# The opening of an encoder trunk: a modulation sum set between two products, and the second half of the tokens squared and partly normed before the last product

## The chip, the cores and the metric

The kernel runs as one program on one core of a Trainium2 chip. A core has a matrix engine (TensorE, PE in the profile, with its weight loads as PEld), a vector engine (VectorE, DVE), an activation engine (ScalarE, ACT), GpSimd (POOL) and SyncE (SP), which here only issues transfers. Each engine works through its own instructions in order and waits for the others by semaphores. The metric is the device time of one execution in microseconds, lower is better.

## The reference

Two layers of a transformer-like encoder over 1024 tokens of width 1024, all in float32, and a final RMS norm. In each layer the tokens are normed and modulated, projected once into the queries, keys and values of three attention groups (A: a 2-D neighbourhood, B: a sliding window, C: dense, with a norm per head and a rotation), the groups' outputs are projected back, and a gated feed-forward network follows. What the change touches is the first layer's first line and the part of the projection that makes group C's queries and keys:

```python
cond = jax.nn.silu(c)
for l in range(DEPTH):
    mod = cond @ w_mod[l] + b_mod[l]
    sh_a, sc_a, gt_a, sh_f, sc_f, gt_f = [m[:, None, :] for m in split_cols(mod, (D,) * 6)]
    h = rms_norm(x, g_attn[l]) * (1 + sc_a) + sh_a
    proj = h @ w_in[l]
    ...
```

So before any product with `h` can run, the shift `sh_a` and the scale `sc_a` have to be had from a vector-matrix product over `w_mod`, and the tokens have to be read, squared and summed.

## The kernel before

Width is cut into 8 blocks of 128 (index n), tokens into 8 tiles of 128 (index t) and two halves of 512. `xt` holds the tokens turned, block by block: 128 channels on the partitions, tokens along the row. `hh` and `hl` hold the normed and modulated `h` as two float32r parts, a rounded one and its remainder, and every weight is split in the same way (`whi` by ScalarE, `wlo` by VectorE or POOL). One product of a block and a tile is therefore three matmuls (`mm3`: hi with hi, lo with hi, hi with lo), accumulated in a PSUM tile. The pool of these tiles holds eight (`bufs=8`), called banks here; all the tiles named ps_... below take one each and take turns in them.

The opening, ahead of the loop over layers, is written out by hand in one order, and `pin` keeps the instructions of TensorE, ScalarE, VectorE and SP in the order of the code. Its pieces:

- `gm_load(i)`, `gemv_half(i)`: the modulation of the first layer comes in four pairs of blocks, p = 0 to 3, each from two loads (i = 2p and 2p+1). Of each load VectorE adds up three rows into `ga`, and TensorE takes the fourth straight into the bank `ps_mod`; at the second load TensorE also sums `ga` over the partitions there, and ScalarE copies the row out (`gr`).
- `gemv_turn(p)`, `gemv_finish(p)`: TensorE turns that row to partitions (`ps_m`), VectorE adds the bias and makes the gain (`vecs`).
- `h_blocks(half, rows, ns)`: for the blocks in ns, VectorE makes `nt` (tokens times gain times 1/rms), ScalarE adds the shift and rounds (`hh`), VectorE makes the remainder (`hl`). `pair_done(p)` is the turn, the finish and the two blocks of the first half of the tokens.
- `c_first(n)`: block n of the C product for the first four tiles, twelve matmuls into four banks `ps_c` that stay taken to the end of the opening. In this document C product n means that call.
- `x_load`, `x_square`, `x_rms`, `x_turn`, `spread`: the tokens of a half are loaded as four tiles `xn`; ScalarE squares them with a running sum (`xt,rx<-xn`; what it writes to `xt` is thrown away) and takes the root, VectorE the reciprocal; TensorE turns each block (`ps_x`) and ScalarE copies it to `xt`; `spread` turns the four columns of 1/rms to rows (`ps_r`). For the first half those rows are copied to `rb`, for the second they are read from the bank.
- `w_split`: the next pair of C weight blocks split; `spill`: `xt` stored to device memory by SP; `turn_vecs`: the second layer's vectors turned (`pst`); `c_norm_first`: the start of the C norm of token tile 0 (`gm`, `cq`, then POOL's rotation `ct`).

The layer's loop then begins with the C product of token tiles 4 and 5, which needs the second half's `hh` and `hl`, and goes on with the A and B projections (`ps_ab`, weights split by VectorE and later by POOL), the C norms of tiles 1 to 7 (`csq`, `r`, `cq`, `ct`, `qn`) and the turns of the normed tiles (`pq`, `pk`). The order of VectorE, ScalarE and POOL is pinned there too.

All engine calls pass through one recording helper, so nearly every row of the profile says L49; the tiles' names tell the rows apart.

Of the kernel before, what the change touches and what calls it, by code (L numbers as in the profile page):

```python
# [10 lines left out]
F32 = mybir.dt.float32  # L11
# [8 lines left out]
P = 128  # L20
D = 1024
S = 1024
KC = D // P
# [62 lines left out]
def trunk(ctx: ExitStack, tc, A, C, out):  # L86
# [358 lines left out]
    def spread(r, j0, psp, tag="mm"):  # L445

        ps = psp.tile([P, 512], F32, name="ps_r", tag=tag)
        for j in range(4):
            pe.transpose(
                ps[:, j * P : (j + 1) * P], bc(r[:, j0 + j : j0 + j + 1], [P, P]), ident  # L450
            )
        return ps
# [83 lines left out]
    st_cm, stp = open_pool("start", side="right")  # L536
# [32 lines left out]
    def x_rms(r):  # L569
        act.activation(r, r, AF.Sqrt, bias=epst, scale=1.0 / D)  # L570
        dve.reciprocal(r, r)

    def x_turn(half, xn, ns, engines):

        c = slice(half * H, (half + 1) * H)
        for n in ns:
            ps = psl.tile([P, 512], F32, name="ps_x", tag="mm")
            for i in range(4):
                pe.transpose(
                    ps[:, i * P : (i + 1) * P], xn[i][:, n * P : (n + 1) * P], ident  # L580
                )
            if engines[n % 2] is act:
                act.copy(xt[:, n, c], ps)
            else:
                dve.tensor_copy(xt[:, n, c], ps)
# [23 lines left out]
            rows = A["w_mod"][0, r0 : r0 + 4 * P, c0 : c0 + 2 * P]  # L609
            sp.dma_start(gm[:, :, g, :], rows.rearrange("(k p) n -> p k n", p=P))  # L610

    def gemv_half(i):
        p, s = i // 2, i % 2
        gm = gms.pop(i).rearrange("p k g n -> p k (g n)")
        if s == 0:
            gas[p] = stp.tile([P, 4 * P], F32, name="ga", tag="ga", bufs=2)
            gps[p] = psl.tile([P, 4 * P], F32, name="ps_mod", tag="mm")
        ga, row = gas[p], gps[p][0:1]
        for k in range(3):
            mod_add(4 * s + k, ga, gm[:, k])  # L620
        pe.matmul(row, condT[:, 4 * s + 3 : 4 * s + 4], gm[:, 3], start=(s == 0), stop=False)
        if s:
            pe.matmul(row, ones, ga, start=False, stop=True)
            gas[p] = stp.tile([1, 4 * P], F32, name="gr", tag="gr", bufs=1)
            act.copy(gas[p], row)

    def gemv_turn(p):

        ps = gps[p] = psl.tile([P, 4], F32, name="ps_m", tag="mm")
        row = gas.pop(p)  # L630
        for c in range(4):
            pe.transpose(ps[:, c : c + 1], row[:, c * P : (c + 1) * P], ident[0:1, 0:1])

    def gemv_finish(p):

        ns = slice(2 * p, 2 * p + 2)
        m, v = (t[:, 0:16].rearrange("p (g n) -> p g n", g=2) for t in (mods[0], vecs[0]))
        dve.tensor_tensor(
            out=m[:, :, ns], in0=gps.pop(p).rearrange("p (g n) -> p g n", g=2),
            in1=v[:, :, ns], op=ALU.add,  # L640
        )
        dve.scalar_tensor_tensor(
            out=gsc[0][:, ns], in0=m[:, 1, ns], scalar=1.0,
            in1=vecs[0][:, 48 + 2 * p : 50 + 2 * p], op0=ALU.add, op1=ALU.mult,
        )

    def h_blocks(half, rows, ns):

        c = slice(half * H, (half + 1) * H)
        ts = {}  # L650
        for n in ns:
            t = ts[n] = stp2.tile([P, H], F32, name="nt", tag="nt", bufs=3)
            dve.scalar_tensor_tensor(
                out=t, in0=xt[:, n, c], scalar=gsc[0][:, n : n + 1], in1=rows,
                op0=ALU.mult, op1=ALU.mult,
            )
        for n, t in ts.items():
            act.activation(hh[:, n, c], t, AF.Identity, bias=mods[0][:, n : n + 1])
        for n, t in ts.items():
            dve.scalar_tensor_tensor(  # L660
                out=hl[:, n, c], in0=t, scalar=mods[0][:, n : n + 1], in1=f32(hh[:, n, c]),
                op0=ALU.add, op1=ALU.subtract,
            )
# [4 lines left out]
            sp.dma_start(dst, v)  # L668
        wcs.append(st)

    def c_first(n):

        wh, wl = wC[n // 2]
        for t in range(T0):
            ts_ = slice(t * P, (t + 1) * P)
            mm3(
                pssC[t], hh[:, n, ts_], hl[:, n, ts_], wh[:, n % 2], wl[:, n % 2],
                n == 0, n == KC - 1,
            )
# [52 lines left out]
    def pair_done(p):  # L732
        gemv_turn(p)
        gemv_finish(p)
        if p == 0:
            keep_busy(8)
        h_blocks(0, rb, (2 * p, 2 * p + 1))
# [39 lines left out]
    pair_done(2)  # L777
    x_square(1, 1, xns[1][1], rxs[1])
    c_first(4)
    c_first(5)  # L780
    w_split()
    wab.append(w_ab(0, 1))
    spill(0)
    gemv_half(7)
    pair_done(3)
    for j in (2, 3):
        x_square(1, j, xns[1][j], rxs[1])
    x_rms(rxs[1])
    x_turn(1, xns[1], range(4), (act, act))
    c_first(6)  # L790
    x_turn(1, xns[1], range(4, KC), (act, act))
    c_first(7)
    spill(1)
    rows = spread(rxs[1], 0, psl)
    turn_vecs(1, v1)
    gm = stp.tile([P, 2048], F32, name="gm", tag="gm", bufs=3)
    first_t1 = c_norm_first(pssC[0], gm[:, 0:512], gm[:, 512:1024], gm[:, 1024:1032])
    for n in range(0, KC, 2):
        h_blocks(1, rows, (n, n + 1))
    sp.dma_start(sinkc, bc(A["sink_sw"].rearrange("l h -> (l h)")[None, :], [P, 12]))  # L800
    for l in range(2):
# [1551 lines left out]
```

## Time and profile before

| | |
|---|---|
| median of 3 runs | 2461.02 us (2459.26 to 2463.18) |
| the profiled execution | 2460.37 us, its span 2458.6 us |
| mean granted TensorE clock | 0.991 |
| busy share TensorE, VectorE, ScalarE, POOL | 97%, 74%, 50%, 31% |
| the opening ends and the layer begins | about 71 us |

Read it so: a row of a timeline has the start and the duration in microseconds, engine, line, operation, the tile written and those read, partitions x elements, how often, and in brackets the idle time ahead of it with what ended it. Rows with x2 or more are merged from neighbours that ran one behind the other. Matmul durations overlap, so the distance from one start to the next is what one costs. All times are from the start of the span.

### The profile page before, as it was taken

The numbers are of one execution on the slowest core, as the hardware profiler recorded it, in microseconds if no ns is written. First come the engines' busy times: TensorE is split into PE (matmuls) and PEld (weight loads), VectorE is DVE, ScalarE is ACT, GpSimd is POOL, SyncE is SP. The second block draws the span as 40 slices with busy tenths as digits, with TensorE's granted clock in tenths as the row PEclk, the third lists the DMA queues.
The fourth block names the chain that finished last, engine by engine and source line by source line (L and its number), as shares of the span: only waits on it lengthen the run. The fifth ranks groups of instructions, "written<-read, shape, count | busy, mean of one in ns | idle before, by whom it ended". The sixth has DMA issues, their size and how long they took to land.

```text
span 2458.6 us, 34285 instructions
## 1 busy us (share of the span) xinstructions
PE 2390.3 (97%) x12005; PEld 1992.7 (81%) x12005; DVE 1821.8 (74%) x2966; ACT 1224.9 (50%) x2306; POOL 764.3 (31%) x769
## 2 busy tenths in 40 slices
PE   8999999999999999999999999999999999999998
PEld 5787899878788877788887789987887888888886
DVE  5757999877967878587677679999698555446865
ACT  3422888954543333344544148888454333333443
POOL 1520444620244444300036114465005434430001
PEclk9999999999999999999999999999999999999999
DMA  8468205245345454496433851151624332229743
GB/s 287 147 177 287 54 14 146 57 151 167 95 142 173 158 168 140 154 287 201 129 116 106 259 195 27 41 152 44 210 90 141 125 115 95 99 102 283 215 134 110
DMA packets 285206, 356.04 MB, mean 145 GB/s; under 512 B 32997, under 2 KB 201533, under 8 KB 285033
## 3 DMA queue, kind: packets, MB, share of 16 engines
q1 hardware_dynamic: 277816, 341.12, 44.6%
q10 hardware_dynamic: 6912, 12.59, 1.6%
q8 instruction: 95, 1.56, 0.3%
q14 instruction: 79, 0.64, 0.1%
q0 software_dynamic: 304, 0.14, 0.0%
HBM read 269.62 MB, written 86.69 MB: 145 GB/s over the span
## 4 chain that ended last, share of the span: by engine, by line
PE 71%; DVE 11%; DMA 6%; issue 5%; ACT 4%; POOL 2%; SPq 1%; ACTq 0%; POOLq 0%; DVEq 0%
PE ps_w L49 30%; PE ps_d L49 10%; PE ps_o L49 7%; PE pv L49 6%; PE ps_ab L49 5%; PE T L49 4%; PE sC L49 3%; DVE wpt L49 2%; DMA wmt<-in_w_mod_dram 2%; PE ps_c L49 1%; ACT pr L49 1%; DMA zt<-skA 1%; PE sA L49 1%; DMA zAd<-zt 1%; DMA w<-in_w_down_dram 1%
## 5 line engine op out<-in xcount | busy, mean ns | idle before, releaser
L49 PE MATMUL ps_d<-wpt 128*128 128x512 f32 x1848 | 425.3, 390 | 2.0 <-DVE wpt L49 0.7
L49 PEld LDWEIGHTS ps_d<-wpt 128*128 128x128 f32 x1848 | 345.4, 188 | 77.2 <-DVE wpt L49 3.1
L49 POOL TENSOR_SCALAR pr<-pr,rs 128x1024 f32<-128x1024 f32 (+4 forms) x252 | 207.6, 826 | 308.5 <-DVE rs L49 290.7
L49 POOL TENSOR_TENSOR sg<-sg,u 128x512 f32<-128x512 f32 x86 | 124.2, 1445 | 360.9 <-ACT sg L49 228.0
L49 PE MATMUL pv<-pt,vs 128*128 128x256 f32 x1216 | 202.5, 297 | 8.0 <-DVE rs L49 2.3
L49 DVE TENSOR_TENSOR pt<-T,pt 128x512 fp32r<-128x512 f32 x304 | 199.4, 680 | 11.4 <-ACT pt L49 9.9
L49 ACT CAST pt<-T 128x512 fp32r<-128x512 f32 x304 | 170.2, 586 | 44.5 <-PE T L49 42.8
L49 PE MATMUL T<-identr,pr 128*128 128x128 f32 x1288 | 187.6, 273 | 2.2 <-ACT rb L49 1.0
L49 ACT COPY u<-ps_w 128x512 f32<-128x512 f32 x128 | 75.2, 587 | 215.1 <-PE ps_w L49 215.1
L49 PEld LDWEIGHTS pv<-pt,vs 128*128 128x128 f32 x1216 | 161.7, 190 | 23.2 <-DVE y L49 7.6
L49 DVE SCALAR_TENSOR_TENSOR acc<-wmt,condT,acc 128x512 f32<-128x512 f32 (+1 forms) x98 | 115.0, 1183 | 84.5 <-DMA wmt<-in_w_mod_dram 84.2
L49 DVE TENSOR_TENSOR wpt<-w,wpt 128x512 fp32r<-128x512 f32 x154 | 111.2, 722 | 84.0 <-ACT wpt L49 83.9
L49 PEld LDWEIGHTS T<-identr,pr 128*128 128x128 f32 x1288 | 153.1, 141 | 21.9 <-issue 3.2
L49 POOL TENSOR_TENSOR wpt<-ws,wpt 128x512 fp32r<-128x512 f32 x80 | 112.3, 1405 | 181.5 <-ACT wpt L49 139.3
L49 ACT CAST wpt<-w 128x512 fp32r<-128x512 f32 x154 | 95.5, 620 | 134.2 <-PE ps_d L49 127.9
L49 ACT CAST wpt<-ws 128x512 fp32r<-128x512 f32 x176 | 107.8, 622 | 56.4 <-issue 22.4
L49 ACT CAST wpt<-graw 128x512 fp32r<-128x512 f32 x154 | 95.0, 617 | 74.6 <-DMA graw<-gpd 65.2
L49 DVE TENSOR_TENSOR wpt<-ws,wpt 128x512 fp32r<-128x512 f32 x96 | 85.1, 895 | 59.1 <-ACT wpt L49 59.0
L49 DVE TENSOR_REDUCE rs<-sC 128x1 f32<-128x1024 f32 x96 | 116.4, 1218 | 6.4 <-PE sC L49 5.9
L49 DVE TENSOR_TENSOR wpt<-graw,wpt 128x512 fp32r<-128x512 f32 x154 | 110.4, 717 | 10.5 <-ACT wpt L49 10.4
L49 PE MATMUL ps_w<-ht3h,wpt 128*128 128x512 f32 x352 | 111.8, 399 | 6.4 <-ACT sg L49 6.4
L49 DVE TENSOR_TENSOR ws<-wr 128x512 f32<-128x512 f32 x88 | 78.8, 898 | 51.7 <-POOL wpt L49 48.7
(287 smaller groups left out, 6027.3 us busy)
## 6 DMA issues: line engine op xcount, KB each, us to landing
wr<-in_w_gu_dram SPq DMA_DIRECT2D x92, 512.0 KB, 4.2
gpd<-sg SPq DMA_DIRECT2D x154, 256.0 KB, 4.4
graw<-gpd SPq DMA_DIRECT2D x76, 512.0 KB, 3.7
w<-in_w_down_dram SPq DMA_DIRECT2D x110, 256.0 KB, 5.2
wmt<-in_w_mod_dram SPq DMA_DIRECT2D x48, 512.0 KB, 5.9
qk<-qkd SPq DMA_DIRECT2D x44, 512.0 KB, 7.3
wst<-in_w_o_dram SPq DMA_DIRECT2D x32, 512.0 KB, 3.5
wmt<-in_w_mod_dram SPq DMA_DIRECT2D x64, 256.0 KB, 3.5
```

The source lines that it names most:

```text
L49: ins = op(*args, **kwargs)
```

## The change

It moves calls of the opening's hand-written order and splits two functions so that they can be called in pieces.

1. `gemv_half(7)`, the last modulation sum, is called between C products 4 and 5, and without its copy; the copy (`gemv_row`), the turn and the finish are called apart, and C product 5 is issued as two pieces of two token tiles, one ahead of the turn and one behind it.
2. The last two squares of the second tokens and their root and reciprocal stand ahead of that copy.
3. The spread of their 1/rms stands ahead of C product 6.
4. Their blocks 0 and 1 are normed behind product 6, blocks 2 and 3 behind product 7, and only blocks 4 to 7 behind the start of the C norm.

```diff
--- before.py
+++ after.py
@@ -609,7 +609,7 @@
             rows = A["w_mod"][0, r0 : r0 + 4 * P, c0 : c0 + 2 * P]
             sp.dma_start(gm[:, :, g, :], rows.rearrange("(k p) n -> p k n", p=P))
 
-    def gemv_half(i):
+    def gemv_half(i, copy=True):
         p, s = i // 2, i % 2
         gm = gms.pop(i).rearrange("p k g n -> p k (g n)")
         if s == 0:
@@ -621,8 +621,13 @@
         pe.matmul(row, condT[:, 4 * s + 3 : 4 * s + 4], gm[:, 3], start=(s == 0), stop=False)
         if s:
             pe.matmul(row, ones, ga, start=False, stop=True)
-            gas[p] = stp.tile([1, 4 * P], F32, name="gr", tag="gr", bufs=1)
-            act.copy(gas[p], row)
+            if copy:
+                gemv_row(p)
+
+    def gemv_row(p):
+        row = gps[p][0:1]
+        gas[p] = stp.tile([1, 4 * P], F32, name="gr", tag="gr", bufs=1)
+        act.copy(gas[p], row)
 
     def gemv_turn(p):
 
@@ -668,10 +673,10 @@
             sp.dma_start(dst, v)
         wcs.append(st)
 
-    def c_first(n):
+    def c_first(n, ts=None):
 
         wh, wl = wC[n // 2]
-        for t in range(T0):
+        for t in ts or range(T0):
             ts_ = slice(t * P, (t + 1) * P)
             mm3(
                 pssC[t], hh[:, n, ts_], hl[:, n, ts_], wh[:, n % 2], wl[:, n % 2],
@@ -777,25 +782,31 @@
     pair_done(2)
     x_square(1, 1, xns[1][1], rxs[1])
     c_first(4)
-    c_first(5)
+    gemv_half(7, copy=False)
     w_split()
     wab.append(w_ab(0, 1))
     spill(0)
-    gemv_half(7)
-    pair_done(3)
     for j in (2, 3):
         x_square(1, j, xns[1][j], rxs[1])
     x_rms(rxs[1])
+    gemv_row(3)
+    c_first(5, (0, 1))
+    gemv_turn(3)
+    c_first(5, (2, 3))
+    gemv_finish(3)
+    h_blocks(0, rb, (6, 7))
     x_turn(1, xns[1], range(4), (act, act))
+    rows = spread(rxs[1], 0, psl)
     c_first(6)
+    h_blocks(1, rows, (0, 1))
     x_turn(1, xns[1], range(4, KC), (act, act))
     c_first(7)
     spill(1)
-    rows = spread(rxs[1], 0, psl)
+    h_blocks(1, rows, (2, 3))
     turn_vecs(1, v1)
     gm = stp.tile([P, 2048], F32, name="gm", tag="gm", bufs=3)
     first_t1 = c_norm_first(pssC[0], gm[:, 0:512], gm[:, 512:1024], gm[:, 1024:1032])
-    for n in range(0, KC, 2):
+    for n in (4, 6):
         h_blocks(1, rows, (n, n + 1))
     sp.dma_start(sinkc, bc(A["sink_sw"].rearrange("l h -> (l h)")[None, :], [P, 12]))
     for l in range(2):
```

What that does on the engines is shown at three places. First TensorE, at C product 5, with the buffers' numbers left in (ps_c_297 to ps_c_300 are the four tiles' banks). Before, the end of product 5 and what follows:

```order
L49 MATMUL ps_c_299<-whi_405,hh_106 128x512
L49 MATMUL ps_c_299<-whi_405,hl_107 128x512
L49 MATMUL ps_c_299<-wlo_406,hh_106 128x512
L49 MATMUL ps_c_300<-whi_405,hh_106 128x512
L49 MATMUL ps_c_300<-whi_405,hl_107 128x512
L49 MATMUL ps_c_300<-wlo_406,hh_106 128x512
L49 MATMUL ps_mod_435<-gm_360,condT_84 1x512
L49 MATMUL ps_mod_435<-ga_434,onesr_78 1x512
L49 MATMUL ps_m_501<-identr_68,gr_499 128x1 x4
```

And in the changed kernel, the same place, which now begins right behind product 4:

```order
L49 MATMUL ps_mod_435<-gm_360,condT_84 1x512
L49 MATMUL ps_mod_435<-ga_434,onesr_78 1x512
L49 MATMUL ps_c_297<-whi_405,hh_106 128x512
L49 MATMUL ps_c_297<-whi_405,hl_107 128x512
L49 MATMUL ps_c_297<-wlo_406,hh_106 128x512
L49 MATMUL ps_c_298<-whi_405,hh_106 128x512
L49 MATMUL ps_c_298<-whi_405,hl_107 128x512
L49 MATMUL ps_c_298<-wlo_406,hh_106 128x512
L49 MATMUL ps_m_499<-identr_68,gr_491 128x1 x4
L49 MATMUL ps_c_299<-whi_405,hh_106 128x512
```

The sum `ps_mod` stands ahead of the product and the turn `ps_m` in its middle; the turned blocks `ps_x` follow the product at once.

Second VectorE, from the remainder of the fifth and sixth block on (the difference, - before and + after; `ga` is the sum over loads, `wlo` the weight split, `ps_r` the spread 1/rms of the second tokens):

```order
-L49 TENSOR_TENSOR wlo<-wst,whi 128x1024
 L49 SCALAR_TENSOR_TENSOR ga<-gm,condT,ga 128x512 x3
+L49 TENSOR_TENSOR wlo<-wst,whi 128x1024
+L49 RECIPROCAL rx<-rx 128x4
 L49 TENSOR_TENSOR vecs_85<-ps_m,vecs_85 128x2x2
 L49 SCALAR_TENSOR_TENSOR vecs_85<-vecs_85 128x2
 L49 SCALAR_TENSOR_TENSOR nt<-xt,vecs_85,rb 128x512 x2
 L49 SCALAR_TENSOR_TENSOR hl<-nt,vecs_85,hh 128x512 x2
-L49 RECIPROCAL rx<-rx 128x4
+L49 SCALAR_TENSOR_TENSOR nt<-xt,vecs_85,ps_r 128x512 x2
+L49 SCALAR_TENSOR_TENSOR hl<-nt,vecs_85,hh 128x512 x2
```

The three additions of the last load have passed the weight split, the reciprocal has passed the finish of the last pair, and the second tokens' blocks stand right behind the first tokens' last ones.

Third ScalarE, from the split of the last C weights on (`xt,rx<-xn` are the squares, `xt<-ps_x` the copies of turned blocks):

```order
 L49 CAST whi<-wst 128x1024
+L49 ACTIVATE xt,rx<-xn 128x2x512 x2
+L49 ACTIVATE rx<-rx,epst 128x4
 L49 COPY gr<-ps_mod 1x512
 L49 ACTIVATE hh<-nt,vecs_85 128x512 x2
-L49 ACTIVATE xt,rx<-xn 128x2x512 x2
-L49 ACTIVATE rx<-rx,epst 128x4
-L49 COPY xt<-ps_x 128x512 x8
+L49 COPY xt<-ps_x 128x512 x4
+L49 ACTIVATE hh<-nt,vecs_85 128x512 x2
+L49 COPY xt<-ps_x 128x512 x4
+L49 ACTIVATE hh<-nt,vecs_85 128x512 x2
```

The squares and the root have passed the copy `gr`, and the eight copies of turned blocks have the second tokens' `hh` between and behind them. SP's transfers and POOL's instructions keep their order.

## The prediction

> **What bounds the kernel now.** First the page: TensorE is busy nearly throughout, so a gain must come from the places where it waits.
>
> ```profile
> span 2458.6 us, 34285 instructions
> ...
> PE 2390.3 (97%) x12005; PEld 1992.7 (81%) x12005; DVE 1821.8 (74%) x2966; ACT 1224.9 (50%) x2306; POOL 764.3 (31%) x769
> ```
>
> Then a table by stage of the opening and of the layer's start, cut where the chain of waits changes hands; the columns are the stretch and its length, the busy time of TensorE, its weight loads, VectorE, ScalarE and POOL (with instructions), the granted clock, the DMA share and GB/s. It shows which engine is full: ScalarE in 62 to 71, VectorE in 71 to 86 while TensorE holes, TensorE again from 116.8 to 142.2.
>
> ```profile
> 62.00:71.00 9.00, 8.60 (x45) 6.59 (x45) 1.58 (x3) 7.49 (x15) 0.00 (x0) 1.00 0.72 268
> 71.00:86.20 15.20, 10.41 (x36) 7.95 (x35) 14.16 (x22) 6.49 (x10) 4.71 (x4) 0.78 0.41 133
> 86.20:116.80 30.60, 29.87 (x156) 24.38 (x154) 25.64 (x43) 13.26 (x35) 20.64 (x18) 1.00 0.44 118
> 116.80:142.20 25.40, 25.40 (x136) 21.27 (x137) 21.16 (x29) 9.98 (x21) 16.50 (x13) 1.00 0.39 113
> ```
>
> Third, TensorE's timeline through the opening. The reader is to see the order (C product 4 to row 54.15, product 5, the last modulation sum and its turn, four turned blocks, product 6, four turned blocks, product 7, spread, vectors) and where it stands still: 0.72 before 59.60, 0.29 inside product 6, 4.41 before 75.48, 0.73 before 116.78.
>
> ```profile
> 54.15 0.39 PE L49 MATMUL ps_c<-whi,hh 128*128 128x512 f32 x1
> 57.00 1.02 PE L49 MATMUL ps_mod<-gm,condT 128*1 128x512 f32 x2
> 59.60 0.40 PE L49 MATMUL ps_m<-identr,gr 1*128 1x1 f32 x4 [0.72 <-ACT gr L49]
> 59.94 1.97 PE L49 MATMUL ps_x<-identr,xn 128*128 128x128 f32 x16
> 62.79 0.50 PE L49 MATMUL ps_c<-whi,hl 128*128 128x512 f32 x1 [0.29 <-DVE hl L49]
> 65.69 2.12 PE L49 MATMUL ps_x<-identr,xn 128*128 128x128 f32 x16
> 67.57 0.48 PE L49 MATMUL ps_c<-whi,hh 128*128 128x512 f32 x1
> 70.41 0.60 PE L49 MATMUL ps_r<-identr,rx 128*128 128x128 f32 x4
> 70.84 0.23 PE L49 MATMUL pst<-identr,v 72*128 72x72 f32 x1
> 75.48 0.79 PE L49 MATMUL ps_c<-whi,hh 128*128 128x512 f32 x1 [4.41 <-ACT hh L49]
> 89.59 0.39 PE L49 MATMUL ps_ab<-hh,whi 128*128 128x512 f32 x1
> 95.03 0.79 PE L49 MATMUL pq<-identr,qn 128*128 128x128 f32 x8
> ```
>
> ```profile
> 116.78 0.50 PE L49 MATMUL ps_ab<-hh,wlo 128*128 128x512 f32 x1 [0.73 <-POOL wlo L49]
> ```
>
> The 4.41 us are VectorE's: after the last product it runs the start of the first C norm (71.25 to 73.93) and only then the second tokens' four pairs of blocks (nt, then hl, 73.93 to 86.25). The table's casts (t5h, 86.25), the next weight split and everything after it stand behind them in VectorE's order.
>
> ```profile
> 60.44 1.42 DVE L49 SCALAR_TENSOR_TENSOR nt<-xt,vecs,rb 128x512 f32<-128x512 f32 x2
> 71.25 0.68 DVE L49 TENSOR_REDUCE gm<-gm 128x8 f32<-128x512 f32 x1
> 73.93 1.40 DVE L49 SCALAR_TENSOR_TENSOR nt<-xt,vecs,ps_r 128x512 f32<-128x512 f32 x2
> 77.66 1.39 DVE L49 SCALAR_TENSOR_TENSOR nt<-xt,vecs,ps_r 128x512 f32<-128x512 f32 x2
> 80.51 1.40 DVE L49 SCALAR_TENSOR_TENSOR nt<-xt,vecs,ps_r 128x512 f32<-128x512 f32 x2
> 86.25 0.15 DVE L49 CAST t5h<-t 32x6 fp32r<-32x6 f32 x1
> 91.92 1.44 DVE L49 TENSOR_TENSOR qn<-ct,qn 128x384 fp32r<-128x384 f32 x2 [0.77 <-ACT qn L49]
> ```
>
> **The change part by part.** No instruction is added or removed and no transfer changes its place in SP's or POOL's order; all is order on TensorE, VectorE and ScalarE. ScalarE's rows there now:
>
> ```profile
> 50.71 1.03 ACT L49 CAST whi<-wst 128x1024 fp32r<-128x1024 f32 x1
> 58.97 0.58 ACT L49 COPY gr<-ps_mod 1x512 f32<-1x512 f32 x1 [7.23 <-PE ps_mod L49]
> 62.52 1.05 ACT L49 ACTIVATE xt<-xn 128x1024 f32<-128x1024 f32 x1
> 64.87 0.30 ACT L49 ACTIVATE rx<-rx,epst 128x4 f32<-128x4 f32 x1
> 65.07 3.98 ACT L49 COPY xt<-ps_x 128x512 f32<-128x512 f32 x8
> 68.88 0.67 ACT L49 ACTIVATE gm<-ps_c 128x512 f32<-128x512 f32 x1
> 74.70 1.38 ACT L49 ACTIVATE hh<-nt,vecs 128x512 fp32r<-128x512 f32 x2 [2.44 <-DVE nt L49]
> ```
>
> *Edit 1, the sum between products.* Its two multiplies move from 57.00 to just behind product 4, 54.15 plus some 0.1. VectorE's three ga steps now stand ahead of the split, so the sum is not late. By rows 57.00 and 58.97 the copy gr starts 1.97 after the first multiply, 56.2, and ends 0.63 later (59.60 less 58.97), 56.85. TensorE meanwhile runs two tiles of product 5: 56.0 to 57.4 (2.85 for twelve matmuls by 57.00 less 54.15). The turn ps_m starts at 57.45 without the 0.72 wait: 2.15 earlier than 59.60. nt follows 0.84 later (60.44 less 59.60), 58.3; hl is whole for its first block 2.35 after nt (62.79 less 60.44), at 60.65. The turn (0.40), the other two tiles (1.4) and the turned blocks (1.97, row 59.94) run on TensorE till 61.3, so the hole before 62.79 goes too.
>
> *Edit 2, squares and 1/rms ahead of gr.* The two squares and the root (62.52 to the first copy at 65.07: 2.55) go to where ScalarE is free, behind the split of 50.71, in the 7.23 that row 58.97 waited; so they end at about 54.4, ahead of 56.2. Their cover is that idle; without it gr would be late by what they overrun. They leave the copies xt, which then start behind the two hh: 58.3, 0.77 for the first nt (74.70 less 73.93 below) and 1.38, so at 60.4 in place of 65.07.
>
> *Edit 3, spread ahead of product 6.* The spread's four turns cost TensorE 0.43 (70.41 to 70.84) and move from behind product 7: nothing in the sum of TensorE's work. They need one bank, freed by the first copy at about 61.0; TensorE is there at 61.3. Product 6 runs 61.75 to 64.5 (2.75: twelve at 0.23). The next turned blocks have three free banks rather than four, since the spread holds one to the end; a copy takes 0.5 (3.98 for eight), a block's turns 0.47 (1.88 for four, 65.69 to 67.57), so the fourth block finds the first bank free: nothing, at worst 0.6. They end at 66.45, product 7 ends 2.84 later (67.57 to 70.41), 69.3, and the turn of the vectors, now directly behind, starts at 69.35 against 70.84: 1.5 earlier.
>
> *Edit 4, blocks 0 to 3 normed early.* Two of the four VectorE pairs move into 62 to 69.3, where VectorE is 1.58 busy in 9.00. What they queue ahead of: ScalarE's hh stands between the copies, so the copies of blocks 4 to 7 wait for nt, and hh of blocks 2, 3 for the copies. The first two nt start when the spread has ended, 61.9; their hh run from 62.7 to 64.1, when no block is turned yet. The last copy ends 0.6 after the last turned block, 67.1; hh of blocks 2 and 3 take 1.38 behind it, to 68.5; the last hl ends 0.8 later, 69.3, when TensorE just gets there and has twelve matmuls of blocks 0 and 1 ahead. The square of the C norm ends 0.67 behind hh (row 68.88), 69.15, against VectorE's need of it at 69.75. That is the thinnest cover of the change, 0.6 us; ScalarE's busy 7.49 in 9.00 becomes about 8. From 69.75 VectorE runs as from 71.25, with two pairs: the first costs 3.73 beside POOL's rotation (73.93 to 77.66), the second 2.87 like the last two now (80.51 to 86.25 for both). The step of row 86.25 then comes 1.5 + 5.74 earlier (the vectors' 1.5, and the two pairs gone, 80.51 to 86.25): **7.2 us**.
>
> *What TensorE makes of it.* It starts on the second tokens at 69.5 and needs 48 matmuls (89.59 less 75.48 now) at 2.85 per twelve, 11.4, plus some 0.5 for hl of block 5: 81.3 against 89.59, 8.3 earlier. That is 1.1 more than VectorE gives. The half clock of 77 to 81 is not in these rows' rate and falls away with the hole before it. The turn of the first normed tile (95.03) now has 1.67 to spare behind VectorE's qn (91.92 plus 1.44); 0.6 stay. From there to 116 the longest of VectorE's waits in total is for ScalarE's qn, behind its own rows; the others are under half a us:
>
> ```profile
> DVE qn L49 <- ACT qn L49: 3.9, 5, 0.8
> ```
>
> So that stretch moves as one by 7.2 with POOL's split at its end; TensorE, 8.3 early, meets it with a wait of 0.73 + 1.1, about 1.8: this is where the rest of its lead is late next. Behind it TensorE is full (25.40 of 25.40), and the stage after that starts from its last turn, as the chain of waits has it:
>
> ```profile
> 141.40 0.63 PE pq L49 x8
> 142.24 0.35 SPq L49
> ```
>
> No transfer there hangs on anything but that turn, so the shift is kept to the end.
>
> **The sum.** 1.5 + 5.74 = 7.2 off the profiled execution's 2460.37 (span 2458.6 and 1.8 around it): 2453.2. The median of the runs is 0.65 above that execution, so 2453.8. Bounds: if VectorE did not hold the stretch to 116, TensorE's 8.3 and the 0.73 would count, 9.0; if the early pairs brought nothing, 1.5 stays.
>
> [...] TensorE was given half its clock twice in the opening.
>
> ```profile
> 47.00:49.20 2.20, 0.21 (x4) 0.12 (x3) 1.80 (x5) 0.82 (x2) 0.00 (x0) 1.00 0.15 38
> 50.60:54.00 3.40, 3.40 (x10) 2.66 (x9) 2.19 (x3) 1.15 (x3) 0.00 (x0) 0.50 0.19 52
> 77.30:81.30 4.00, 4.00 (x11) 3.09 (x10) 3.87 (x7) 1.39 (x3) 1.58 (x1) 0.50 0.48 148
> 193.00:200.00 7.00, 4.63 (x21) 3.53 (x20) 6.86 (x10) 0.60 (x1) 0.29 (x2) 1.00 1.05 343
> ```
>
> The first time came behind an idle time of 2 us with narrow sums ahead of it; a hole of as long in 193 to 200 (4.63 busy in 7.00) brought none. The second, behind the 4.41 wait, should vanish; the split and turn that follow were VectorE's to release, so I count nothing for it. The new hole of 1.8 is a doubt: by the row of 50.60 it could cost 3.40 x 0.5 = 1.7, so 2455.5; by that of 193 nothing. [...]
>
> **The rivals.** *The stretch behind 86 does not follow.* If something other than VectorE's order sets POOL's split, such as the weight rows that SP loads there, only 1.5 is kept: 2459.5. For it: the DMA share of 0.44 and a chain that passes through loads. Against: VectorE's list above has no DMA in it, and it is busy 25.64 of 30.60. *TensorE sets that stretch*: 9.0, 2452.0; against it is the 0.73 wait on POOL that is there already. [...]
>
> **How the numbers follow.** 0.2% is 4.9 us, about what a measurement of this kernel tells from no change. Chances: the forecast 0.62 (2453.8, itself within some 2 us by the runs' spread of 2459.26 to 2463.18), TensorE sets the stretch 0.06, a half-clock window in the new hole 0.05, the stretch does not follow 0.19, half clock throughout or slower otherwise 0.08. The first three are faster, 0.73; the fourth is the same; the last is slower. The range goes from 2450.0 (TensorE's case less 2) to 2459.8, which leaves out the slower case and the upper half of the fourth; the likeliest alone would be 2451.5 to 2456.
>
> **What would show it.** ps_m near 57.5, ps_r near 61.3, no TensorE wait of over 1 us from there to the second tokens' end; VectorE's t5h near 79; the wait for POOL's split grown to nearly 2 us; the mA load near 135. I am wrong if the early hh hold back the copies (a TensorE wait at the turned blocks), if the C norm's square comes late, or if the wait for POOL's split stays near 116.

## The result and the profile after

| | before | changed |
|---|---|---|
| median of the runs side by side (11 and 11) | 2457.29 us (2454.73 to 2463.18) | 2451.34 us (2445.28 to 2458.39) |
| ratio of the runs, 95% interval | 1 | 0.997 [0.9959, 0.998] |
| the same against 18 and 19 other runs of before | 1 | 0.9962 [0.9945, 0.998], 0.9973 [0.9959, 0.9987] |
| span of the profiled execution | 2458.6 us | 2445.4 us |
| its mean granted clock | 0.991 | 0.995 |

By the ratio the change takes 7.4 us off (0.003 of 2457.3; 4.9 to 10.1). The spans differ by 13.2, and that is not all the change: by difference some 6 us of it belong to these two executions (the last section). All runs of this study taken together give 2457.9 us as the mean of before (100 runs, standard error 0.35) and 2451.35 as that of the changed kernel (31 runs, 0.69): 6.5 us, uncertain by 0.8.

The page of the changed kernel, to be held against the span line and busy line of before:

```profile
span 2445.4 us, 34284 instructions
...
PE 2382.9 (97%) x12005; PEld 1989.4 (81%) x12005; DVE 1820.0 (74%) x2966; ACT 1224.5 (50%) x2306; POOL 763.6 (31%) x769
```

The table by stage, cut at the same places of the program (first turned blocks, second tokens' product, the step t5h, POOL's split, the mA load; columns as before):

```profile
58.50:67.20 8.70, 8.70 (x55) 7.54 (x54) 6.50 (x10) 7.50 (x14) 0.00 (x0) 1.00 1.06 402
67.20:77.00 9.80, 9.62 (x42) 7.21 (x40) 9.09 (x16) 3.82 (x6) 4.76 (x4) 1.00 0.74 250
77.00:106.90 29.90, 28.54 (x150) 23.23 (x148) 24.95 (x43) 13.13 (x35) 20.85 (x18) 1.00 0.45 122
106.90:132.40 25.50, 25.50 (x136) 21.37 (x137) 21.27 (x29) 10.12 (x21) 16.49 (x13) 1.00 0.39 114
```

The stage that was 15.20 long with TensorE 10.41 busy at a clock of 0.78 is now 9.80 long, with 9.62 busy at 1.00. VectorE's 6.50 busy in the first row (it was 1.58) come mostly from the two block pairs that came forward. The third stage's TensorE idle is its wait at POOL's split. TensorE's rows, from the sum behind product 4 on:

```profile
52.35 1.20 PE L49 MATMUL ps_mod<-gm,condT 128*1 128x512 f32 x2
55.91 0.40 PE L49 MATMUL ps_m<-identr,gr 1*128 1x1 f32 x4
57.73 1.91 PE L49 MATMUL ps_x<-identr,xn 128*128 128x128 f32 x16
59.48 0.62 PE L49 MATMUL ps_r<-identr,rx 128*128 128x128 f32 x4
62.70 1.93 PE L49 MATMUL ps_x<-identr,xn 128*128 128x128 f32 x16
67.23 0.23 PE L49 MATMUL pst<-identr,v 72*128 72x72 f32 x1
67.25 0.48 PE L49 MATMUL ps_c<-whi,hh 128*128 128x512 f32 x1
79.07 0.39 PE L49 MATMUL ps_ab<-hh,whi 128*128 128x512 f32 x1
...
106.88 0.50 PE L49 MATMUL ps_ab<-hh,wlo 128*128 128x512 f32 x1 [1.36 <-POOL wlo L49]
```

No row has a wait until 106.88 (one of 0.2 within the second tokens' product apart): the 0.72, the 0.29 and the 4.41 are gone, and the wait at POOL's split has grown from 0.73 to 1.36. VectorE at the same place:

```profile
60.20 1.40 DVE L49 SCALAR_TENSOR_TENSOR nt<-xt,vecs,ps_r 128x512 f32<-128x512 f32 x2 [0.50 <-PE ps_r L49]
66.03 1.42 DVE L49 SCALAR_TENSOR_TENSOR hl<-nt,vecs,hh 128x512 fp32r<-128x512 f32 x2 [1.56 <-ACT hh L49]
67.64 0.68 DVE L49 TENSOR_REDUCE gm<-gm 128x8 f32<-128x512 f32 x1
70.31 1.40 DVE L49 SCALAR_TENSOR_TENSOR nt<-xt,vecs,ps_r 128x512 f32<-128x512 f32 x2
71.85 2.32 DVE L49 SCALAR_TENSOR_TENSOR hl<-nt,vecs,hh 128x512 fp32r<-128x512 f32 x2
74.09 1.39 DVE L49 SCALAR_TENSOR_TENSOR nt<-xt,vecs,ps_r 128x512 f32<-128x512 f32 x2
76.95 0.15 DVE L49 CAST t5h<-t 32x6 fp32r<-32x6 f32 x1
```

ScalarE's copy of the sum's row, its square for the C norm, and SP's load of mA:

```profile
54.45 0.57 ACT L49 COPY gr<-ps_mod 1x512 f32<-1x512 f32 x1 [1.82 <-PE ps_mod L49]
66.48 0.61 ACT L49 ACTIVATE gm<-ps_c 128x512 f32<-128x512 f32 x1
```

```profile
132.33 0.35 SPq L49 DMA_DIRECT2D mA<-const_maskA_dram  x1
```

The executions begin differently by a us or two, so steps are compared from the end of C product 4 on, which is the last point ahead of all that moved (54.15 before, 52.35 in the changed kernel):

| us from the end of product 4 | ps_ab (TensorE) | t5h (VectorE) | mA (SP) |
|---|---|---|---|
| before | 35.44 | 32.10 | 88.09 |
| changed, three executions | 26.54 to 26.72 | 24.45 to 24.60 | 79.85 to 79.98 |
| only the sum between the products | 34.37 | 31.34 | 86.73 |
| only the second tokens' part | 28.72 | 26.61 | 82.01 |
| all but the four early blocks | 32.88 | 30.08 | 85.47 |
| changed, eight VectorE steps added | 30.32 | 29.72 | 85.44 |
| before, its hole filled | 33.97 | 32.10 | 87.50 |

### The profile page after: what moved, and what is told of

It is laid out like the page before. It is cut to its first block, busy times and chain, and to the rows that moved or that the text cites. A ratio compares the mean times of both kernels' runs of the same rounds, so it can differ in the third digit from the quotient of the medians.

```text
span 2445.4 us, 34284 instructions
## 1 busy us (share of the span) xinstructions
PE 2382.9 (97%) x12005; PEld 1989.4 (81%) x12005; DVE 1820.0 (74%) x2966; ACT 1224.5 (50%) x2306; POOL 763.6 (31%) x769
## 3 DMA queue, kind: packets, MB, share of 16 engines
q8 instruction: 95, 1.56, 0.3%
## 4 chain that ended last, share of the span: by engine, by line
PE 72%; DVE 9%; DMA 6%; issue 5%; ACT 4%; POOL 2%; SPq 1%; ACTq 0%; POOLq 0%; DVEq 0%
PE ps_w L49 32%; PE ps_d L49 10%; PE ps_o L49 7%; PE pv L49 6%; PE ps_ab L49 5%; PE T L49 4%; PE sC L49 3%; PE ps_c L49 1%; DVE wpt L49 1%; ACT pr L49 1%; DMA w<-in_w_down_dram 1%; DMA wmt<-in_w_mod_dram 1%; PE ps_v L49 1%; DMA zt<-skA 1%; DMA zAd<-zt 1%
```

## The experiments

The theory was that VectorE's order sets the opening's end and the 55 us behind it. The rivals: that something else sets that stretch, so that most of the gain is lost there; that TensorE's hole and clock are what counts; and that chance in the clock makes the difference.

**One part at a time.** Three kernels, and the one behind them, share the time runs of before (35). What was expected of these four counts t5h and mA from the start of product 4, some 5 us ahead of its end. The first takes edit 1 alone:

```diff
     c_first(4)
-    c_first(5)
+    gemv_half(7, copy=False)
     ...
-    gemv_half(7)
-    pair_done(3)
+    gemv_row(3)
+    c_first(5, (0, 1))
+    gemv_turn(3)
+    c_first(5, (2, 3))
+    gemv_finish(3)
+    h_blocks(0, rb, (6, 7))
```

> Only edit 1 on the kernel before (the last modulation sum between C products 4 and 5; squares, spread and all eight second-token blocks where they were). Times are counted from the first matmul of C product 4, since the head ahead of it is common to all kernels and differed by 1.7 us between the two profiles: the table casts (t5h) stood at 37.1 before and 29.5 after, the first SP load of the next stage (mA) at 93.1 and 84.9. Theory (VectorE's order from the C norm on sets the layer's start, and the sum only brings the vectors' turn earlier by 1.5): t5h near 35.5, mA near 91.5, the median 1.5 us under before. Rival (the moved sum carries most of the gain, since it takes the waits ahead of the turn away): t5h under 33, the median 4 us or more under before.

Measured: ratio 0.9996 [0.9986, 1.0006], t5h 0.8 earlier and not 1.5. The opening itself was 2.0 earlier (the vectors' copy 14.96 behind product 4 in place of some 17), but VectorE lost 1.2 of it in the first pair of the second tokens, which took 4.96 from nt to nt (71.08 to 76.04) where before needs 3.73. The small step on the sinks took 0.72 there (0.17 in before) and the remainder 2.97 (2.27); the last section shows what held them. VectorE's rows there:

```profile
71.08 1.40 DVE L49 SCALAR_TENSOR_TENSOR nt<-xt,vecs,ps_r 128x512 f32<-128x512 f32 x2
72.52 0.72 DVE L49 TENSOR_SCALAR sinkc<-sinkc 128x12 f32<-128x12 f32 x1
73.15 2.97 DVE L49 SCALAR_TENSOR_TENSOR hl<-nt,vecs,hh 128x512 fp32r<-128x512 f32 x2
76.04 1.39 DVE L49 SCALAR_TENSOR_TENSOR nt<-xt,vecs,ps_r 128x512 f32<-128x512 f32 x2
```

The second takes the squares, the spread and the early blocks, and leaves the sum behind product 5:

```diff
     c_first(4)
     c_first(5)
     ...
-    gemv_half(7)
-    pair_done(3)
+    gemv_half(7, copy=False)
     ...
+    gemv_row(3)
+    gemv_turn(3)
+    gemv_finish(3)
+    h_blocks(0, rb, (6, 7))
     x_turn(1, xns[1], range(4), (act, act))
+    rows = spread(rxs[1], 0, psl)
     c_first(6)
+    h_blocks(1, rows, (0, 1))
     ...
-    rows = spread(rxs[1], 0, psl)
+    h_blocks(1, rows, (2, 3))
     ...
-    for n in range(0, KC, 2):
+    for n in (4, 6):
         h_blocks(1, rows, (n, n + 1))
```

> Edits 2 to 4 without edit 1 (the sum stays behind C product 5; squares and 1/rms ahead of its copy, spread ahead of product 6, blocks 0 to 3 normed early). Theory: the two early pairs bring their 5.7, less some 0.4 to 1.2 because the spread now waits for the first copy of a turned block: t5h near 31.7 to 32.5 from the start of product 4, mA near 87 to 88, the median 5 us under before. Rival (the early blocks only work together with the moved sum, because ScalarE is full without it): TensorE waits of over 2 us at the turned blocks, t5h over 34, the median under 3 us below before.

Measured: 0.9984 [0.9972, 0.9996], so 3.9 us off (1.0 to 6.9), t5h 5.5 earlier. This part carries most of the change. Without the early sum the spread comes too soon for the bank it needs, as TensorE's row says:

```profile
63.20 0.65 PE L49 MATMUL ps_r<-identr,rx 128*128 128x128 f32 x4 [1.23 <-ACT xt L49]
```

The parts give 0.8 and 5.5 at t5h, together 6.3, and both at once 7.5. The 1.2 between is not that wait of 1.23, though the size is the same, but what the first kernel lost in its slow first pair. From the end of product 4 to the turn of the vectors (pst) it is 16.69 before, 14.70 with the sum alone, 16.88 with this part alone and 14.88 with both: the sum is worth 2.0 either way, and this part moves the turn by 0.2 later. From the turn to t5h it is 15.41, 16.64, 9.73 and 9.72, and 15.41 with the sum early and the blocks late (the next kernel): the early blocks are worth 5.7 either way, and only the first kernel stands 1.2 behind.

The third is the changed kernel with the four blocks put back behind the C norm:

```diff
-    h_blocks(1, rows, (0, 1))
     ...
-    h_blocks(1, rows, (2, 3))
     ...
-    for n in (4, 6):
+    for n in range(0, KC, 2):
         h_blocks(1, rows, (n, n + 1))
```

> The changed kernel with only edit 4 undone (all eight second-token blocks behind the start of the C norm; sum, squares and spread stay moved). Theory: the vectors' turn stays early, the 5.7 of two pairs are gone: t5h near 35 to 35.5 from the start of product 4, TensorE's hole of 4 us and a half-clock stretch back, median 1.5 to 2 us under before. Rival (the gain is the hole's and the half clock's, not the pairs'): not told apart by t5h, but then mA comes back by more than t5h does.

Measured: 0.9996 [0.9985, 1.0007], t5h 2.0 earlier than before, which is the early sum. The hole is back at its old length, as TensorE's row shows, so it hangs on where these four blocks stand and on nothing else that was moved:

```profile
71.53 0.79 PE L49 MATMUL ps_c<-whi,hh 128*128 128x512 f32 x1 [4.41 <-ACT hh L49]
```

**VectorE delayed again.** The changed kernel with eight more nt steps, whose result nobody reads, ahead of t5h:

```diff
     for n in (4, 6):
         h_blocks(1, rows, (n, n + 1))
+    for _ in range(8):
+        pad_ = stp2.tile([P, H], F32, name="nt", tag="nt", bufs=3)
+        dve.scalar_tensor_tensor(
+            out=pad_, in0=xt[:, 0, 0:H], scalar=gsc[0][:, 0:1], in1=rb,
+            op0=ALU.mult, op1=ALU.mult,
+        )
```

> The changed kernel with eight more VectorE instructions of 128x512, about 0.76 us each, 6.1 us in all, between the last block's remainder and the table casts; their output is not used. Theory (that stretch moves as one with VectorE's order to POOL's split): t5h near 35.6 from the start of product 4, POOL's split and mA later by about 6 too (mA near 91), the time back near before. Rival 1 (the stretch does not follow VectorE but loads): t5h later by 6, mA by under 2. Rival 2 (TensorE sets the stretch): mA later by 6.1 less its slack, under 4.5.

Measured: 1.0004 [0.9993, 1.0015], which is the level of before; t5h 5.1 and mA 5.5 later than in the changed kernel. VectorE's row, then TensorE's, which has a new hole where the next weights are split:

```profile
77.33 5.39 DVE L49 SCALAR_TENSOR_TENSOR nt<-xt,vecs,rb 128x512 f32<-128x512 f32 x8
```

```profile
83.23 0.79 PE L49 MATMUL ps_ab<-hh,whi 128*128 128x512 f32 x1 [3.63 <-ACT whi L49]
84.49 0.79 PE L49 MATMUL ps_ab<-hh,wlo 128*128 128x512 f32 x1 [0.47 <-DVE wlo L49]
```

5.39 of VectorE's time put in (6.1 was expected) came out as 5.5 at mA 55 us later. From t5h to mA the changed kernel, the three parts and this one take 55.38 to 55.72: the stretch follows VectorE.

**The hole filled in the kernel before.** This tells VectorE's order from TensorE's loss:

```diff
     def turn_vecs(l, v):
     ...
         dve.tensor_copy(vecs[l], pst[:, :72])
+        return pst
     ...
-    turn_vecs(1, v1)
+    keep = turn_vecs(1, v1)
+    for _ in range(16):
+        pe.matmul(keep, identr, bc(identr[:, None, :], [P, 4, P]), start=True, stop=True)
```

> The kernel before, with sixteen extra matmuls of 128x512 on TensorE behind the turn of the vectors, written over the bank of that turn, which nobody reads any more: they fill some 3.7 us of the wait of 4.41 ahead of the second tokens' C product, and nothing else is moved in the opening. The half clock of 74.5 to 81.3 should go with the hole. This tells two accounts of the change's gain apart. Theory (VectorE's order sets the stretch): TensorE starts the second tokens' product when it did, 21.3 us behind the end of product 4, runs it at full clock and ends some 2.2 us earlier (11.4 plus 0.5 in place of 14.1, ps_ab near 33.2 behind the end of product 4 where it was 35.44), but t5h stays at 31.5 to 32.1 and mA at 87.5 to 88.1 behind the end of product 4, the wait for POOL's split grows from 0.73 to 2.5 or more, and the time is 0.9995 to 1.0005. Rival (what the change took away was TensorE's loss, the hole with its half clock, and its clock is worth time by itself): mA comes 2 us or more earlier, near 85.5, and the ratio is 0.999 or less.

The scheduler also interleaved the two tiles of the second tokens' product differently, with the same work. TensorE's and VectorE's rows, and the stretch of 74 to 82 of this kernel and of before:

```profile
69.53 3.92 PE L49 MATMUL pst<-identr 128*128 128x512 f32 x16 [0.33 <-DVE vecs L49]
...
114.37 0.50 PE L49 MATMUL ps_ab<-hh,wlo 128*128 128x512 f32 x1 [1.45 <-POOL wlo L49]
```

```profile
84.43 0.15 DVE L49 CAST t5h<-t 32x6 fp32r<-32x6 f32 x1
```

```profile
74.00:82.00 8.00, 7.47 (x30) 5.01 (x29) 7.73 (x11) 2.98 (x5) 2.98 (x3) 1.00 0.26 80
```

```profile
74.00:82.00 8.00, 6.14 (x15) 4.50 (x16) 7.74 (x12) 3.47 (x6) 4.71 (x4) 0.57 0.50 179
```

The half clock is gone (1.00 for 0.57) and TensorE reaches ps_ab 1.5 sooner, but t5h stands at 32.10 as before, mA at 87.50, and the wait at POOL's split has doubled to 1.45 (2.5 or more was expected, but TensorE gained 1.5 and not 2.2, and the split itself came 0.6 sooner). So in the opening the hole was the mark of VectorE's lateness, not a price of its own. The time is 0.9993 [0.9983, 1.0002]: 1.7 us off, from 4.2 off to 0.5 on. The time alone does not rule out the rival's 2 us, but its mA near 85.5 did not come. The 0.6 that mA gained is not the clock's either: the execution before lost it in one slow pair of VectorE behind t5h (told below). Whether full clock there brings a little behind mA stays open.

**What is late next.** Four kernels add to the changed one. The first fills TensorE's two waits of 2 us ahead of products 2 and 4 with five idle matmuls each:

```diff
         if p == 0:
             keep_busy(8)
+        else:
+            keep = psl.tile([P, 4, P], F32, name="ps_keep", tag="mm")
+            for _ in range(5):
+                pe.matmul(keep, identr, bc(identr[:, None, :], [P, 4, P]), start=True, stop=True)
```

> The changed kernel with five unused 128x512 matmuls (1.2 us at full clock) in each of the two 2 us holes ahead of C products 2 and 4. Every profile so far had half-clock windows of about 3.4 us within or behind these holes, one or two of them, 1.4 to 1.7 us of TensorE each. Theory (the idle time brings the window): clock 1.00 from 36 to 58, products 2 to 4 without matmuls of 0.43, the median 1.5 to 3 us under the changed kernel. Rival (a window comes at any rate, at a place given by chance): as many slow matmuls as before, the median the same within 1.5 us.

Measured: 0.9957 [0.9942, 0.9972] where the changed kernel had 0.9962 in the same rounds, 1.2 us less by the ratios and 2.3 by the medians, with 1.5 to 3 expected. The clock from 36 to 58, in this kernel and then in the changed one:

```profile
36.00:58.00 22.00, 20.77 (x89) 12.87 (x90) 16.47 (x26) 11.74 (x20) 1.20 (x1) 1.00 0.68 214
```

```profile
36.00:58.00 22.00, 19.27 (x69) 11.23 (x70) 14.95 (x25) 10.25 (x18) 1.20 (x1) 0.92 0.64 204
```

Part of what that gives is lost at once: t5h comes 25.70 behind product 4 in place of 24.60. VectorE now waits for the load of the sinks, which SP issues behind sixteen stores, and runs the slow remainder again:

```profile
70.70 0.17 DVE L49 TENSOR_SCALAR sinkc<-sinkc 128x12 f32<-128x12 f32 x1 [0.65 <-DMA sinkc<-in_sink_sw_dram]
70.78 2.97 DVE L49 SCALAR_TENSOR_TENSOR hl<-nt,vecs,hh 128x512 fp32r<-128x512 f32 x2
```

```profile
54.94 11.54 SPq L49 DMA_DIRECT2D xd<-xt  x16
66.53 0.64 SPq L49 DMA_DIRECT2D cst<-const_rope_dram  x1
67.22 0.65 SPq L49 DMA_DIRECT2D sinkc<-in_sink_sw_dram  x1
```

The next two give one weight split of the first layer to POOL instead of VectorE, alone and with the fills:

```diff
-        w = split_tile(wab.pop(0), KC, (ct, "wx", 2), dve)
+        w = split_tile(wab.pop(0), KC, (ct, "wx", 2), pool if l == 0 else dve)
```

> The changed kernel with the remainder of the first A and B weight split on POOL, which idles there, in place of VectorE (1.23 us). Theory (VectorE's order sets POOL's next split): that split 1.1 us earlier from the end of C product 4 (51.7 now), TensorE's wait of 1.36 ahead of it gone, a new wait of 0.5 to 1 at the first A and B product, mA 0.5 to 0.8 earlier than 80.0. Rival (POOL's own rows set it): the split within 0.3 of 51.7 or later, mA at 80.0 or later.

> Both of the last two edits on the changed kernel, to see whether they beat it: by the theory 2 to 3.5 us under the changed kernel, 9 to 11 under before; by the rivals no more than it gains.

Measured: alone one run, 2448.57 us, within the changed kernel's runs, with mA 79.49 behind product 4; with the fills 0.9962 [0.9948, 0.9976], no better by the ratio than the changed kernel and 1.3 us by the medians, where 2 to 3.5 was expected. TensorE's waits for POOL's splits in the latter:

```profile
77.97 0.50 PE L49 MATMUL ps_ab<-hh,wlo 128*128 128x512 f32 x1 [0.25 <-POOL wlo L49]
104.85 0.50 PE L49 MATMUL ps_ab<-hh,wlo 128*128 128x512 f32 x1 [0.50 <-POOL wlo L49]
```

1.36 became 0.25 and 0.50, but POOL's split itself began only 0.5 sooner behind product 4 (51.19 for 51.67), where 1.1 was expected, and mA came 0.3 to 0.4 sooner. The last one moves the sinks' load ahead of the stores, in the same rounds with the changed kernel once more:

```diff
     sp.dma_start(mB, C["maskB"])
+    sp.dma_start(sinkc, bc(A["sink_sw"].rearrange("l h -> (l h)")[None, :], [P, 12]))
     ...
         h_blocks(1, rows, (n, n + 1))
-    sp.dma_start(sinkc, bc(A["sink_sw"].rearrange("l h -> (l h)")[None, :], [P, 12]))
```

> The kernel with the two holes filled and the weight split on POOL, with one more edit: the load of the sinks (sinkc, 128x12) is issued right behind the load of mB, ahead of the 16 spill stores, where it now stands behind them (66.32 in SP's queue with the fills alone). Theory (VectorE's order sets the step t5h, and with an early opening the next late thing is this load): the wait of 0.65 of sinkc falls away; sinkc starts right behind nt at about 69.9 from the span's start, and t5h comes 24.4 us behind the end of product 4, as with the fills and the split together, also in executions where the load would be late (25.70 with the fills alone). TensorE's clock stays 1.00 from 36 to 58. mA follows at 79.5 behind the end of product 4; time against before 0.995 to 0.9965, at most 1 us better than with the two holes filled and the split. Rival (the slow remainder of 2.3 to 2.97 us, beside POOL's rotation, is what sets t5h, not the load): t5h from product 4 stays between 24.4 and 25.7 however early the load is, and the remainder hl still takes 2.3 or more.

> The changed kernel as it is, once more, in the same rounds as the kernel with all three additions. If the gain of the change is 7 us, its ratio to before lies at 0.997 with an interval of some 0.0015 either way; the profile has t5h 24.5 and mA 79.9 behind the end of product 4, as in its two profiles so far, and at least one window of half clock between 36 and 58. If the additions are worth anything that can be told, the kernel with them is 2 us or more below this one; if the clock's windows come by chance and only move, the two agree within 1.5 us.

Measured: 0.996 [0.9945, 0.9975], and 0.9973 [0.9959, 0.9987] for the changed kernel. The wait of 0.65 was not removed but became one of 0.32 elsewhere: the scheduler puts VectorE's small step as early as its load, now into the finish of the last block pair, and it waits there:

```profile
57.12 0.17 DVE L49 TENSOR_SCALAR sinkc<-sinkc 128x12 f32<-128x12 f32 x1 [0.32 <-DMA sinkc<-in_sink_sw_dram]
57.20 1.41 DVE L49 SCALAR_TENSOR_TENSOR nt<-xt,vecs,rb 128x512 f32<-128x512 f32 x2
```

t5h came at 24.78 and the remainder took 2.33, which is what the rival said (24.4 to 25.7, and 2.3 or more); the theory's 24.4 did not come. (The 66.32 that was expected to hold with the fills alone is of the kernel with fills and split; with the fills alone the load stands at 67.22, as shown.) In these rounds the median with all three additions is 2.7 us below the changed kernel's, where 2 or more was to mean that they are worth something, but the intervals overlap. None of the three kernels with fills can be told from the changed one alone by its own interval. Their 24 runs together have a mean of 2448.4 us (standard error 0.67) against 2451.35 for the changed kernel: 2.9 us lower, uncertain by 1.0, over chips and rounds that were not all shared. That the fills are worth something is likely; that the split or the load adds to it is not shown.

The changed kernel was also taken once more beside the fills:

> The changed kernel a second time, for what is chance. Theory (of the 13 us between the two profiles 8 are the change, the rest half-clock windows that fall differently in each execution): from the end of C product 4 the casts t5h at 24.6 and mA at 80.0 within 0.2 again; the first product's start may differ by up to 2 us, with the clock granted at 20 to 28; the median 6 to 9 us under before. Rival (the early head and the later gain of 3 us belong to the change): span within 1.5 us of 2445 again.

Measured: 2449.91 us median of 8, 0.9962 [0.9945, 0.998]; t5h 24.45 and mA 79.85 behind product 4. So its steps repeat to 0.15 us, though its product 4 ended 2.3 us later (54.63). Its span was 2444.1, within 1.5 of 2445 as the rival said, but not by an early head; in the third execution it was 2448.2, so the near agreement of the first two spans is chance.

## Why the prediction was right in size and wrong in level

*The size.* 7.2 us was forecast and 7.4 measured (6.5 over all runs). The two terms, from the trace: from product 4 to the vectors' turn 16.69 before and 14.88 now, 1.81 where 1.5 stood; from there to t5h 15.41 and 9.72, 5.69 where 5.74 stood. t5h came 7.5 earlier.

*The step that failed* is the last line of the sum, the level it was taken from. I set the profiled execution's 2460.37 against a median of three runs, 2461.02, and took 7.2 from that. Both were high: 100 runs of before have a mean of 2457.9. From there the same sum gives 2450.7, which is 0.6 below the changed kernel's mean. The forecast of 2453.8 lay 2.5 above the measured median, and against the runs of before beside it (2457.29) it showed only 3.5 us of the 7.4. Three runs that agree within 4 us do not give a level to 1 us when the single runs range over 14 (2448.9 to 2462.7 in the 35).

*Terms that were off in size.* The turn ps_m came 3.56 behind product 4, with 3.3 forecast, since the first sums were still at half clock (0.50 granted till 52.75; 1.04 from the first pair to the second, 0.85 in the kernel with the sum alone); no time was lost by it, as ps_r came at 7.13 with 7.15 forecast. The early sum alone brought 0.8 at t5h and not 1.5 (the slow first pair above), though it turned the vectors 2.0 earlier. The wait at POOL's split grew by 0.63 and not by 1.1: TensorE's lead was 8.7 at ps_ab, a little over my 8.3, but the split itself came 8.1 sooner rather than 7.2. Of that 0.3 are at t5h, and 0.6 lie between t5h and mA, where the execution before took 55.99 and the others 55.4 (55.72 with VectorE steps added): one pair of its qn steps, 17.3 us behind t5h, took 2.05 where the same pair takes 1.45 with the hole filled. That part of mA's 8.1 is luck of one execution and no gain of the change.

*The thinnest cover* held: the C norm's square ended at 67.09, and VectorE needed it at 67.64, 0.55 where 0.6 was forecast. The early hh did not hold back the copies of turned blocks. VectorE did wait 1.56 for the second pair's hh, as worked out, at no cost.

*The rivals.* That the stretch behind 86 does not follow fell by the table: mA moved by all of it, and 5.39 put in on VectorE came out as 5.5. That TensorE sets it fell with the filled hole. The half clock in the new hole did not come: the clock was 1.00 on both sides of the 1.36. Half clock throughout fell: 1.00 from 58.5 to 132.4.

*The clock.* I counted nothing for the second half-clock spell; on the opening's path that holds, by the filled hole. I counted nothing for the new hole either, and no run shows a rule by which that had to be so; the runs showed 1.00 on both sides of its 1.36. With each hole of 3.63 to 4.41 us (before, the sum alone, all but the four early blocks, eight VectorE steps added) the half clock lasted 6.7 to 6.9 us (twice 0.43 of 8.00 in the row of 74 to 82 of before), and from 36 to 58, with the waits of 2 us, some 3.5 (twice 0.08 of 22.00) or twice that. How busy TensorE was ahead of it stands in the last section.

## What to carry to other kernels

Set the level of a forecast from many runs, or forecast the difference: the sum of a change may be right to 0.3 us at a step of the trace while the base moves by 3. To tell which engine sets a stretch, add known work to it and see how much comes out at the far end, and fill the other engine's hole and see that nothing does; a hole and its half clock can be as large as here (4.41 us, and 0.57 over the 8 us from 74 to 82) and still be only a mark of another engine's lateness. When parts of a change do not add up, compare them point by point along the trace before a wait of the right size is taken for the cause. When a stage is brought forward, list the transfers that keep their old time: here a load of six numbers per layer, behind sixteen stores, was late next.

## What the runs showed of the hardware that was not expected

**The half clock came in spells of 3.41 us or twice that, at places that differ between executions.** In the clock records of the two profiled executions, before and changed, the half-clock spells begin whole multiples of 3.413 us apart and, until the last matmul, last once or twice that. In the execution of before the waits ahead of products 2 and 4 are both 1.99 us long, but the first lies across two stretches of that length, counted from a spell's start (the first two rows, 2.36 and 2.20 busy), and the second within one (the third, 1.13 busy); the half clock came behind the third alone, in the prediction's row of 50.60:

```profile
33.50:36.92 3.42, 2.36 (x9) 0.58 (x7) 1.24 (x4) 0.58 (x1) 0.00 (x0) 1.00 0.99 345
36.92:40.33 3.41, 2.20 (x8) 1.61 (x9) 2.20 (x4) 3.25 (x5) 0.00 (x0) 1.00 1.05 371
47.16:50.57 3.41, 1.13 (x5) 0.73 (x5) 3.15 (x6) 2.19 (x3) 0.00 (x0) 1.00 0.14 35
```

Counted over the stretches at full clock of these two records, from 10 to 2430 us: where TensorE was busy for 0.43 of the stretch or less, the next one was at half clock 10 times of 10; from 0.47 to 0.50, once in 4; from 0.53 to 0.90, never in 78; and once in the 1309 fuller ones, behind a stretch with a row of sixteen one-column matmuls. So in these records, that one apart, the half clock came behind stretches that were up to 0.47 busy, and of before's two waits of 1.99 us only behind the one that fell within one stretch. The clock from 36 to 58 was 0.92, or 0.84 to 0.85, in all ten profiles without the fills, and 1.00 in the three with them. The hole at 193 to 196 that the prediction set against it lies across two stretches in before (2.81 and 1.64 of 3.41 busy, the clock 1.00 over 180 to 200); in three other executions (changed once more, the sum alone, the fills alone) it was 0.91 there, in one of them with TensorE idle for only 2.26 of the 20. Around the new wait of 1.36 at POOL's split TensorE was busy for 2.05 of 3.41, and the clock stayed at 1.00.

Between executions of one kernel the granted clock differs, and the time with it, by as much as the change is worth: over the changed kernel's 31 runs (0.991 to 0.996) 0.001 of mean clock goes with 2.3 us, over 72 of before's with 2.1. The two profiled executions differ by 0.004, which by these slopes goes with some 9 of their 13.2 us. The slopes are no prices: the half clock that the change removed is 0.001 of the 0.004, and the filled hole shows that up to mA it cost nothing.

The idle matmuls that are to keep the clock up made the execution of before late, where the clock was already down. The eight behind the first pair's turn, in the execution of before (clock 0.58 from 20 to 28) and in the changed kernel's (1.00):

```profile
21.99 3.78 PE L49 MATMUL ps_idle<-identr 128*128 128x512 f32 x8
25.70 1.49 PE L49 MATMUL ps_mod<-gm,condT 128*1 128x512 f32 x2
```

```profile
21.20 2.11 PE L49 MATMUL ps_idle<-identr 128*128 128x512 f32 x8
23.24 1.02 PE L49 MATMUL ps_mod<-gm,condT 128*1 128x512 f32 x2
```

They took 3.78 us in place of 2.11, on top of 0.8 by which they began later, and the real sum behind them came 2.5 later, of which 1.7 was left at the start of product 4. A second execution of the changed kernel had the same (clock 0.57 there), so it is chance and no part of the change.

VectorE's pair of remainders took 1.42 alone, and 2.27 to 2.97 where POOL ran its rotation beside it. In before and in the changed kernel each of the two then ended 0.55 behind the end of the POOL instruction that was running when it began, and with the sum alone and the fills alone the second did so. The pair took 2.97 where the second remainder met POOL's instruction of 1.60, as with the sum alone; in before it met one of 1.17, which ended at 77.19, and the remainder ended at 77.73:

```profile
73.97 1.60 POOL L49 TENSOR_TENSOR ct<-ct 128x512 f32<-128x512 f32 x1
```

```profile
74.36 1.75 DVE L49 SCALAR_TENSOR_TENSOR hl<-nt,vecs,hh 128x512 fp32r<-128x512 f32 x1
```

The small step on the sinks that took 0.72 with the sum alone, where it had no wait for its load, likewise ran beside POOL's rotation (71.25 to 73.90).
